# Context stages of a hybrid RWKV and convolution backbone: ScalarE reads each projection bank twice, VectorE works from a second SBUF tile

## The chip, the cores and the metric

The program runs on one core of one Trainium2 chip. The metric is the device time of one execution in microseconds (us), as the median of several runs. In the text TensorE is also called PE, VectorE DVE, ScalarE ACT, GpSimd POOL and SyncE SP, as the profile calls them. PEld is the loading of weights into TensorE, which overlaps its matmuls.

## The reference

The network has two layers over 512 latent tokens and 256 context tokens of width 1024. Layer 0 is the one that the change touches. It mixes tokens by a two-directional linear recurrence (RWKV-7), beside a short gated convolution. Layer 1 is a convolution module with a long kernel. What matters here of layer 0:

```python
def centred_shift(x):
    p = jnp.pad(x, ((0, 0), (1, 1), (0, 0)))
    return 0.5 * (p[:, :-2] + p[:, 2:])
...
    r = r + (centred_shift(r) - r) * mu_rkv[0]
    k = k + (centred_shift(k) - k) * mu_rkv[1]
    v = v + (centred_shift(v) - v) * mu_rkv[2]
...
    rc, kc, vc, zac, bc, cc, xc, zbc = jnp.split(hc @ w_in, EVEN_SPLITS, axis=-1)
    yac, S_f, S_b = rwkv_seq(rwkv_prep(hc, rc, kc, vc, *rw), zero, zero, r_k, lnx_w, lnx_b, ctx_out)
    r, k, v, za, bg, cg, xb, zb = jnp.split(h @ w_in, EVEN_SPLITS, axis=-1)
    ya, _, _ = rwkv_seq(rwkv_prep(h, r, k, v, *rw), S_f, S_b, r_k, lnx_w, lnx_b, True)
    y = jnp.concatenate([ya.astype(h.dtype) * jax.nn.silu(za), yb * jax.nn.silu(zb)], axis=-1) @ w_out
```

So each of the projections r, k and v is mixed with its left and right neighbour in time: (1 - mu) times itself plus mu/2 times each neighbour. The gate za goes through x * sigmoid(x).

## The kernel before, in words

All of layer 0 works on pairs of heads: 16 heads of 64 channels make 8 pairs of 128 channels, one channel to a partition, with time along the free dimension. A projection of one pair over the 512 latent tokens is 24 matmuls into one PSUM bank (8 blocks of the width, each as high times high, high times low and low times high of a number split in two fp32r parts). Over the 256 context tokens it is 24 shorter ones.

The work runs in 12 stages, `for s in range(12)` near the end of the function. Stages 0 to 3 are the context stages: each runs the recurrence of two head pairs over the context. Stages 4 to 11 do one head pair each over the latents. A stage holds a serial chain over chunks of 64 tokens (`chain_ctx`, `chain_lat`), and a string of letters, `STAGE`, says in what order the work for later stages is written beside it. K and V project k and v of the next two pairs (`prep_ctx`, `project`). L and H prepare the inputs of the recurrence (`light`, `heavy`). S and M invert the small triangular systems (`solve` on VectorE, 31 dependent steps; `merge` on TensorE, tile names mgc and mgl, which needs the result of `solve` in the tiles kdmc and amc, or kdml and aml). F fills in work that only later stages need: `fills` projects r and the gate za of the 8 pairs, by the tables `FILL_R` and `FILL_Z`, and sends them to DRAM.

The order that each engine runs in is not the written one. A scheduler lists the instructions of each engine by its own estimates of when they are ready, and every engine then runs its list strictly in that order. In a list a name ends in what it stands for: plv7 is the PSUM bank of v of pair 7 over the latents, pcv7 the same over the context, plr7 is r, pza7 the gate, pac30 and pal11 score blocks of a state, c2 the third context state and l0 the first latent state.

The change touches two helpers.

- `shifted` (lines 440 to 446) empties the bank of a projection. ScalarE writes (1 - mu) times the bank into the result tile (line 442). Then VectorE twice adds mu/2 times the bank, shifted by one column to the right and to the left (lines 443 and 445). These two read the bank again, so the bank is free after the second of them. `project` calls it once for the context bank, if there is one, and once for the latent bank.
- `gate` (lines 902 to 909) makes z * (1 + tanh(z / 2)): ScalarE reads the bank for the tanh (line 907), VectorE reads the bank again and multiplies (line 908).

The banks of projections alternate between two, mm0 and mm1 (`ps_mm`), so a projection can start when the one before the last has been emptied. The tile with the tag O has one buffer. In the latent stages it holds the output of a state. Before that the modulation's weights pass through it, fetched by `rest`, which counts its calls in `mv["n"]`: there are 17 calls, all of them before the context stages begin. The gate's tile gz also has one buffer, and is free again when its copy to DRAM has landed. These copies are queued on POOL.

Of the kernel before, what the change touches and what calls it, by code (L numbers as in the profile page):

```python
# [10 lines left out]
AF = mybir.ActivationFunctionType  # L11
ALU = mybir.AluOpType
# [6 lines left out]
SEQ = 512  # L19
# [33 lines left out]
def kernel(ctx: ExitStack, tc: tile.TileContext, I: dict, out: bass.AP):  # L53
    nc = tc.nc
    V, S, G, T = nc.vector, nc.scalar, nc.gpsimd, nc.tensor
# [111 lines left out]
    def ps_mm(name):  # L167
        flip["mm"] ^= 1
        return ps.tile([P, 512], F32, tag=f"mm{flip['mm']}", name=name)
# [17 lines left out]
    def w(tag, name, dt=F32):  # L187
        return wk.tile([P, SIZE.get(tag, 512)], dt, tag=tag, name=name, bufs=NBUF.get(tag, 1))
# [4 lines left out]
    def small(name, shape):  # L193
        return cvp.tile(shape, F32, tag=name, name=name)

    omu, hmu, hka, oka = (small(n, [P, k]) for n, k in (("omu", 24), ("hmu", 24), ("hka", 8), ("oka", 8)))
# [232 lines left out]
    def load_w(cb, name):  # L429
        lo_for(name)  # L430
        src = w_in[:, cb * P : (cb + 1) * P].rearrange("(k p) c -> p k c", p=P)
        return [w_half(src[:, 4 * b : 4 * b + 4, :], f"{name}{b}") for b in range(2)]

    def proj(wt, o, h):
        for kt in range(KT):
            ks = slice(kt % 4 * P, kt % 4 * P + P)
            wh, wl = wt[kt // 4]
            mm3(o, wh[:, ks], wl[:, ks], h[0][:, kt, :], h[1][:, kt, :], kt == 0, kt == KT - 1)

    def shifted(pl, res, p, which):  # L440
        j, n = which * 8 + p, pl.shape[1]
        S.activation(res, pl, AF.Copy, scale=omu[:, j : j + 1])
        V.scalar_tensor_tensor(out=res[:, 1:n], in0=pl[:, 0 : n - 1], scalar=hmu[:, j : j + 1],
                               in1=res[:, 1:n], op0=ALU.mult, op1=ALU.add)
        V.scalar_tensor_tensor(out=res[:, 0 : n - 1], in0=pl[:, 1:n], scalar=hmu[:, j : j + 1],
                               in1=res[:, 0 : n - 1], op0=ALU.mult, op1=ALU.add)

    def project(p, which, rc=None, between=None):
        nm = "rkv"[which] + str(p)
        wt = first_w.pop(nm) if nm in first_w else load_w(which * 8 + p, nm)  # L450
        if rc is not None:
            pc = (ps_at if nm in ("k0", "k1", "v0", "v1") else ps_mm)("pc" + nm)[:, :CTX]
            proj(wt, pc, (hch, hcl))
            shifted(pc, rc, p, which)
            if between:
                between()
        pl = ps_mm("pl" + nm)
        proj(wt, pl, hlat)
        flip["at"] ^= 1
        tag = ("cg", "yb")[flip["at"]]  # L460
        rl = cvp.tile([P, SEQ], F32, tag=tag, name="l" + nm)
        shifted(pl, rl, p, which)
        nc.gpsimd.dma_start(psp[p, which], rl)
# [438 lines left out]
    def gate(p, cb, nm):  # L902
        wt = load_w(cb + p, f"{nm}{p}")
        pz = ps_mm(f"p{nm}{p}")
        proj(wt, pz, hlat)
        g = cvp.tile([P, SEQ], F32, tag="gz", name=f"g{nm}{p}")
        S.activation(g, pz, AF.Tanh, scale=0.5)
        V.scalar_tensor_tensor(out=g, in0=g, scalar=1.0, in1=pz, op0=ALU.add, op1=ALU.mult)
        return g

    def finish(st):
# [21 lines left out]
    def fill(p):  # L933
        project(p, 0)
        gz = gate(p, 24, "za")
        nc.gpsimd.dma_start(psp[p, 3], gz)
# [39 lines left out]
    mv = {"n": 0}  # L976
# [49 lines left out]
    def fills(x):  # L1026
        for p in range(8):
            if FILL_R[p] == x:
                project(p, 0)
            if FILL_Z[p] == x:  # L1030
                gz = gate(p, 24, "za")
                nc.gpsimd.dma_start(psp[p, 3], gz)
# [24 lines left out]
    for s in range(12):  # L1057
# [11 lines left out]
        for x in STAGE[(s >= 2) + (s >= 4)]:  # L1069
# [25 lines left out]
            elif x == "C":  # L1095
                conv_branch(s - 3, st["anchor"])
                if s == 10:
                    rs.close()
                    op = rs.enter_context(tc.tile_pool(name="op", bufs=1, reuse_waits="tile", side="right"))
                    env["lo"] = V  # L1100
        if s == 3:
# [3 lines left out]
                                   op0=ALU.add, op1=ALU.mult)  # L1105
# [35 lines left out]
    with ExitStack() as l1:  # L1141
# [14 lines left out]
        def dense(name):  # L1156
            flip["mm"] = (flip["mm"] + 1) % 4
            return bank(name, ("mm0", "mm1", "uh0", "uh1")[flip["mm"]])
# [159 lines left out]
        for m in range(4):  # L1318
            mv = lp.tile([P, 4], F32, tag="mv", name=f"mv{m}", bufs=2)
# [3 lines left out]
            for q in range(2):  # L1323
                V.tensor_scalar(out=cres[m][q], in0=cres[m][q], scalar1=mv[:, 0:1], scalar2=mv[:, 3:4],
                                op0=ALU.subtract, op1=ALU.mult)
# [12 lines left out]
        for j in range(16):  # L1338
            c0 = 2 * EC + j * P
            src = w1_in[:, c0 : c0 + P].rearrange("(k p) c -> p k c", p=P)  # L1340
            pz = dense(f"pz{j}")
# [21 lines left out]
        for n in range(2):  # L1363
# [10 lines left out]
            for j in range(16):  # L1374
                if j % 2 == 0:
                    src = w2[j * P : (j + 2) * P, sl].rearrange("(a p) c -> p a c", p=P)
# [4 lines left out]
            for m in range(4):  # L1381
# [6 lines left out]
                if n == 0:  # L1388
                    V.tensor_tensor(out=sv, in0=acc[m], in1=gn, op=ALU.mult)
                    V.tensor_scalar(out=ssq[:, 2:3], in0=ssq[:, 0:1], scalar1=1.0 / D, scalar2=RMS_EPS,  # L1390
                                    op0=ALU.mult, op1=ALU.add)
# [87 lines left out]
```

## Time and profile before

| what | value |
|---|---|
| median of 3 runs | 1378.45 us (1374.93 to 1384.68) |
| the profiled execution's own time | 1377.51 us |
| its span, from the first to the last instruction | 1375.7 us |
| mean TensorE clock granted | 0.994 of full speed |
| TensorE, VectorE, ScalarE, GpSimd busy | 1315.9, 985.7, 743.1, 127.3 us |
| context stages with the first latent preparation, about | 150 to 470 us of the span |

The span is 1.8 us shorter than the execution's own time. What is worked out from the trace is set against the profiled execution, which lies 0.94 us under the median. A page of the profile gives each engine's busy time, and a chain that is followed back from the last instruction. The views of the trace used below are the waits (who waited for whom, how long, how often), the timeline of one engine (start, duration, what, and in square brackets the idle time before it and what ended it), the durations of one source line (smallest, median and largest, in ns), and windows (busy time of each engine in a stretch).

### The profile page before, as it was taken

The page shows a single profiled execution, that of the slowest core. Times are in us where ns is not written, and L with a number is a line of the kernel's source. Part 1 is how long each engine was busy: PE and PEld are TensorE (multiplying, and loading weights), DVE is VectorE, ACT ScalarE, POOL GpSimd, SP SyncE. Part 2 cuts the span into 40 slices and gives each one's busy share as a digit, 9 for nine tenths or more (in the row PEclk, how much of TensorE's full clock was granted, in tenths as well). Part 3 has the DMA queues.
Part 4 walks back from the last instruction along what each step waited for, and adds up shares of the span by engine and source line. Part 5 has one row for each costly group of instructions (what it writes and reads, how often), then busy time and mean ns, then how long its engine had stood idle before and what let it go on. Part 6 is the DMA issues. An engine that isn't in the chain of part 4 may idle for free.

```text
span 1375.7 us, 29697 instructions
## 1 busy us (share of the span) xinstructions
PE 1315.9 (96%) x11925; PEld 974.2 (71%) x11925; DVE 985.7 (72%) x2304; ACT 743.1 (54%) x1509; POOL 127.3 (9%) x263
## 2 busy tenths in 40 slices
PE   6999999999999999999999989999999999999998
PEld 2657677777667766666666666687787787788886
DVE  5857889767999699999999988458653653644323
ACT  6456466445765576675756745548741431654222
POOL 4142200001101010101101000010000000000000
PEclk9999999999999999999999999999999999999999
DMA  9965522222323322223222221678521321233232
GB/s 332 274 218 199 161 63 72 92 76 72 98 92 107 100 63 65 86 65 90 68 73 85 70 73 48 199 260 294 189 82 42 122 81 42 64 119 94 92 102 82
DMA packets 139754, 158.54 MB, mean 115 GB/s; under 512 B 15503, under 2 KB 104223, under 8 KB 139497
## 3 DMA queue, kind: packets, MB, share of 16 engines
q1 hardware_dynamic: 123152, 106.47, 24.9%
q0 software_dynamic: 15856, 49.12, 10.9%
q8 instruction: 93, 1.52, 0.5%
q10 hardware_dynamic: 608, 1.06, 0.2%
q14 instruction: 45, 0.37, 0.1%
HBM read 138.33 MB, written 18.28 MB: 114 GB/s over the span
## 4 chain that ended last, share of the span: by engine, by line
PE 49%; DVE 11%; ACT 7%; issue 4%; DMA 3%; POOL 0%; SPq 0%; DVEq 0%; ACTq 0%; POOLq 0%
PE pu L58 13%; PE pz L58 6%; PE f L58 6%; PE pxb L58 3%; PE o L58 3%; PE uh L58 3%; PE pcg L58 3%; DVE E L693 2%; PE pzb L58 1%; PE zol L58 1%; PE onl L58 1%; PE pc L58 1%; PE px L58 1%; DMA wr<-in_ev_w_out_dram 1%; PE plr L58 1%
## 5 line engine op out<-in xcount | busy, mean ns | idle before, releaser
L58 PE MATMUL o<-wh,y 128*128 128x512 f32 x248 | 79.7, 396 | 0.0
L752 DVE TENSOR_TENSOR xtmpl<-Xl,Yl 128x126 f32<-128x126 f32 (+22 forms) x248 | 62.6, 252 | 3.1
L754 DVE TENSOR_TENSOR Yl<-Yl,xtmpl 128x126 f32<-128x126 f32 (+22 forms) x248 | 62.5, 252 | 2.8
L1292 ACT CAST ah<-a 64x512 fp32r<-64x512 f32 x32 | 19.8, 618 | 74.1 <-DVE a L1287 73.7
L58 PEld LDWEIGHTS uh<-UV,BKt 128*64 128x64 f32 x704 | 26.4, 137 | 38.6 <-ACT UV L881 27.9
L58 PEld LDWEIGHTS o<-wh,y 128*128 128x128 f32 x248 | 46.2, 188 | 9.4
L58 PE MATMUL o<-wl,y 128*128 128x512 f32 x124 | 49.6, 400 | 1.5 <-DVE wl L131 1.5
L58 PE MATMUL pal<-ARl,BKl 64*128 64x128 f32 x512 | 43.9, 290 | 5.9 <-DVE E L693 2.6
L881 ACT COPY UV<-uh 64x128 f32<-64x128 f32 x128 | 33.2, 260 | 27.6 <-PE uh L58 25.3
L131 DVE TENSOR_TENSOR wl<-wr,wh 128x1024 fp32r<-128x1024 f32 x28 | 34.2, 1223 | 19.1 <-ACT wh L130 18.9
L1287 DVE TENSOR_TENSOR a<-pu,a 128x512 f32<-128x512 f32 x16 | 11.0, 690 | 49.5 <-PE pu L58 47.2
L58 PE MATMUL uh<-UV,BKt 128*64 128x64 f32 x704 | 36.6, 232 | 10.2 <-ACT UV L881 4.9
L58 PEld LDWEIGHTS pal<-ARl,BKl 64*128 64x128 f32 x512 | 34.5, 187 | 15.8 <-issue 6.3
L693 DVE TENSOR_TENSOR E<-pal,maskE 128x512 f32<-128x512 f32 x64 | 42.9, 686 | 0.4 <-PE pal L58 0.2
L1244 DVE SCALAR_TENSOR_TENSOR pr<-px,dbe,What 119x512 f32<-119x512 f32 x32 | 22.6, 746 | 26.6 <-PE px L58 26.6
L130 ACT CAST wh<-wr 128x1024 fp32r<-128x1024 f32 x28 | 29.6, 1056 | 18.9 <-DMA wr<-in_ev_w_out_dram 9.7
L58 PEld LDWEIGHTS uh<-Ol,E 64*64 64x64 f32 x512 | 20.3, 133 | 25.8 <-ACT Ol L874 23.9
L888 DVE SCALAR_TENSOR_TENSOR Hl<-uh,PCl,HPl 128x64 f32<-128x64 f32 x112 | 26.2, 276 | 13.2 <-ACT UV L881 5.0
L754 DVE TENSOR_TENSOR Yc<-Yc,xtmpc 128x126 f32<-128x126 f32 (+22 forms) x124 | 31.5, 254 | 3.2
L752 DVE TENSOR_TENSOR xtmpc<-Xc,Yc 128x126 f32<-128x126 f32 (+22 forms) x124 | 31.5, 254 | 3.1
L842 ACT ACTIVATE HPl<-Hl,PCl 128x64 f32<-128x64 f32 x96 | 28.1, 340 | 9.4 <-DVE Hl L888 8.4
L58 PEld LDWEIGHTS zol<-Hl,ARl 64*64 64x64 f32 x448 | 18.0, 134 | 20.8 <-DVE Yl L754 5.9
(1003 smaller groups left out, 4278.7 us busy)
## 6 DMA issues: line engine op xcount, KB each, us to landing
wr<-in_ev_w_out_dram SPq DMA_DIRECT2D x28, 512.0 KB, 5.2
mwr<-in_mod_w_dram POOLq DMA_DIRECT2D x28, 256.0 KB, 4.1
wrv<-in_ev_w_in_dram SPq DMA_DIRECT2D x16, 256.0 KB, 3.5
ectx<-in_mod_w_dram POOLq DMA_DIRECT2D x16, 256.0 KB, 4.2
wrr<-in_ev_w_in_dram SPq DMA_DIRECT2D x16, 256.0 KB, 2.8
wrza<-in_ev_w_in_dram SPq DMA_DIRECT2D x16, 256.0 KB, 2.9
wrcg<-in_ev_w_in_dram SPq DMA_DIRECT2D x16, 256.0 KB, 2.9
wrxb<-in_ev_w_in_dram SPq DMA_DIRECT2D x16, 256.0 KB, 3.1
```

Of the source, the lines that this page charges most:

```text
L58: env["pe"] = T.matmul(o, lhsT, rhs, start=start, stop=stop)
L130: S.copy(hi, raw)
L131: env["lo"].tensor_tensor(out=lo, in0=raw, in1=hi, op=ALU.subtract)
L693: st["ev"].append(V.tensor_tensor(out=E[:, h, z * NLAT + c0 : z * NLAT + c0 + m, :], in0=pas[h], in1=maskE[:, z * (1 + h) : z * (1 + h) + ...
L752: V.tensor_tensor(out=tv, in0=X[:, :i, i : i + 1].to_broadcast([P, i, m]), in1=Y[:, i : i + 1, c0:].to_broadcast([P, i, m]), op=ALU.mult)
L754: V.tensor_tensor(out=Y[:, :i, c0:], in0=Y[:, :i, c0:], in1=tv, op=ALU.add)
L842: S.activation(t[:, z, :], H[:, z, :], AF.Copy, scale=st["PC"][z][:, i : i + 1])
L881: u_ = S.copy(UV[ZR[1 - h], i : 2 * nch - i : 2 * nch - 1 - 2 * i, ZR[h]], uh[ZR[1 - h], 0:2, :])
L888: h_ = V.scalar_tensor_tensor(out=Hn[:, z, :], in0=uh[:, 2 + z, :], scalar=PC[z][:, i : i + 1], in1=HP[:, z, :], op0=ALU.mult, op1=ALU.add)
L1244: V.scalar_tensor_tensor(out=pr[s][:NPROD], in0=px[s][:NPROD], scalar=dbe[:, 0:1], in1=What[:, n * 512 : n * 512 + 512], op0=ALU.add, op1= ...
L1287: V.tensor_tensor(out=a, in0=pp[1], in1=a, op=ALU.mult)
L1292: S.copy(ahl[s][hr], a[hr])
```

## The change

From the seventeenth call of `rest` on, that is in the context stages, `shifted` has ScalarE read the bank a second time. It writes mu/2 times the bank into a second tile in the one buffer of tag O, and VectorE adds that tile, shifted by one column each way, with two plain additions. VectorE no longer reads the bank. Likewise `gate` has ScalarE copy the bank of za to the second tile, and VectorE multiplies from there. The projections and gates before this point, and the gates zb of the latent stages, stay as they were.

```diff
     def shifted(pl, res, p, which):
         j, n = which * 8 + p, pl.shape[1]
         S.activation(res, pl, AF.Copy, scale=omu[:, j : j + 1])
-        V.scalar_tensor_tensor(out=res[:, 1:n], in0=pl[:, 0 : n - 1], scalar=hmu[:, j : j + 1],
-                               in1=res[:, 1:n], op0=ALU.mult, op1=ALU.add)
-        V.scalar_tensor_tensor(out=res[:, 0 : n - 1], in0=pl[:, 1:n], scalar=hmu[:, j : j + 1],
-                               in1=res[:, 0 : n - 1], op0=ALU.mult, op1=ALU.add)
+        if mv["n"] < 17:
+            V.scalar_tensor_tensor(out=res[:, 1:n], in0=pl[:, 0 : n - 1], scalar=hmu[:, j : j + 1],
+                                   in1=res[:, 1:n], op0=ALU.mult, op1=ALU.add)
+            V.scalar_tensor_tensor(out=res[:, 0 : n - 1], in0=pl[:, 1:n], scalar=hmu[:, j : j + 1],
+                                   in1=res[:, 0 : n - 1], op0=ALU.mult, op1=ALU.add)
+            return
+        sh = w("O", f"sh{which}{p}{n}")[:, :n]
+        S.activation(sh, pl, AF.Copy, scale=hmu[:, j : j + 1])
+        V.tensor_tensor(out=res[:, 1:n], in0=sh[:, 0 : n - 1], in1=res[:, 1:n], op=ALU.add)
+        V.tensor_tensor(out=res[:, 0 : n - 1], in0=sh[:, 1:n], in1=res[:, 0 : n - 1], op=ALU.add)
...
         S.activation(g, pz, AF.Tanh, scale=0.5)
-        V.scalar_tensor_tensor(out=g, in0=g, scalar=1.0, in1=pz, op0=ALU.add, op1=ALU.mult)
+        src = pz
+        if nm == "za" and mv["n"] == 17:
+            src = w("O", f"sh{nm}{p}")[:, :SEQ]
+            S.copy(src, pz)
+        V.scalar_tensor_tensor(out=g, in0=g, scalar=1.0, in1=src, op0=ALU.add, op1=ALU.mult)
         return g
```

In the built program 24 calls of `shifted` (8 over the context, 16 over the latents) and 8 gates have the second read. The scheduler, which now sees the banks freed by ScalarE, also lists other work in another order, on all engines, from the first of them to the end of the first convolution in stage 3. After that the orders are the same again. Three places follow, as they stand in the lists.

TensorE around the merge of the third context state, before the change (pac300 are score blocks, plv7 the last projection of v, mgc2 the merge):

```order
L58 MATMUL pcv7_3538<-hctx_122,wlv71_3534 128x256
L58 MATMUL pac3001_3597<-ARc30_3274,BKc30_3275 128x64
...
L58 MATMUL pac3000_3596<-ARc30_3274,BKc30_3275 128x64
L58 MATMUL zoc2_0_3744<-UV000_1218,ectx_123 64x64 x4
L58 MATMUL mgc2_3386<-amc2_3378,ectx_123 32x32 x32
L58 MATMUL plv7_3566<-hlh0_117,whv70_3527 128x512
...
L58 MATMUL mgc2_3386<-kdmc2_3377,Pmc2_3379 32x32 x32
L58 MATMUL plv7_3566<-hlh0_117,wlv70_3528 128x512
```

The same place of the change:

```order
L58 MATMUL pcv7_3578<-hctx_122,wlv71_3574 128x256
L58 MATMUL plv7_3608<-hlh0_117,whv70_3567 128x512
...
L58 MATMUL plv7_3608<-hlh0_117,wlv70_3568 128x512
L58 MATMUL mgc2_3422<-amc2_3414,ectx_123 32x32 x32
L58 MATMUL plv7_3608<-hlh1_447,whv71_3573 128x512
...
L58 MATMUL mgc2_3422<-kdmc2_3413,Pmc2_3415 32x32 x32
L58 MATMUL plv7_3608<-hlh1_447,whv71_3573 128x512
...
L58 MATMUL pac3001_3641<-ARc30_3310,BKc30_3311 128x64
```

Twelve matmuls of plv7 moved ahead of the merge, nine stand between its halves, and the score blocks moved behind it. The merge of the second context state moved in the same way.

ScalarE at the second copies, of the change (sh26512 is the second tile of v of pair 6 over 512 tokens; before, the rows of the sh tiles were not there):

```order
L442 ACTIVATE lv6_3559<-plv6_3534,omu_99 128x512
L615 ACTIVATE Pc31_3328<-Pc31_3328 128x528
L450 ACTIVATE sh26512_3561<-plv6_3534,hmu_100 128x512
L617 COPY PCc31_3333<-Pc31_3328 128x8
L648 COPY BKc31_3341<-BKc31_3341 64x8x64
L442 ACTIVATE vc3_3491<-pcv7_3578,omu_99 128x256
L771 COPY ectx_123<-kdmc2_3413 32x16x32 x2
L130 CAST whr21_3752<-wrr21_3751 128x512
L780 COPY Pmc2_3415<-mgc2_3422 32x512
L450 ACTIVATE sh27256_3604<-pcv7_3578,hmu_100 128x256
```

The second read of a bank need not stand right behind the first: it stands where the second tile is thought to be free.

VectorE at the end of the inversion of the first latent state, before the change (Xl1 is the transposed input of the next inversion, E110 a score block after its mask):

```order
L693 TENSOR_TENSOR E110_4729<-pal1111_4944,maskE_107 128x512
L752 TENSOR_TENSOR xtmpl0_4788<-Xl0_4786,Yl0_4787 128x70
L445 SCALAR_TENSOR_TENSOR lr7_5183<-plr7_5158,hmu_100,lr7_5183 128x511
...
L754 TENSOR_TENSOR Yl0_4787<-Yl0_4787,xtmpl0_4788 128x16
L746 STREAM_TRANSPOSE Xl1_5640<-Nt_111 128x32x32
L760 STREAM_TRANSPOSE kdml0_4853<-Yl0_4787 128x32x16
L761 STREAM_TRANSPOSE aml0_4854<-kdml0_4853 128x512
```

The same place of the change:

```order
L760 TENSOR_TENSOR Yl0_4843<-Yl0_4843,xtmpl0_4844 128x16
L131 TENSOR_TENSOR wlxb01_5300<-wrxb01_5298,whxb01_5299 128x512
L766 STREAM_TRANSPOSE kdml0_4909<-Yl0_4843 128x32x16
L699 TENSOR_TENSOR E110_4785<-pal1101_4988,maskE_107 128x512
L767 STREAM_TRANSPOSE aml0_4910<-kdml0_4909 128x512
L771 COPY E100_4207<-kdml0_4909 32x16x32 x2
L131 TENSOR_TENSOR wlbg00_5336<-wrbg00_5334,whbg00_5335 128x512
L452 TENSOR_TENSOR lr7_5245<-sh07512_5247,lr7_5245 128x511
L780 COPY Pml0_4911<-mgl0_4918 32x512
L699 TENSOR_TENSOR E110_4785<-pal1110_4999,maskE_107 128x512
```

The second addition for lr7, two of the masked blocks and the transposition Xl1 moved behind the last step of the inversion's transposition aml0, for which the merge of that state waits.

## The prediction

> **What bounds the kernel now.** I read the page's busy times first, then the chain that ended last, then the busy time of each engine in the stretch that the change touches.
>
> ```profile
> PE 1315.9 (96%) x11925; PEld 974.2 (71%) x11925; DVE 985.7 (72%) x2304; ACT 743.1 (54%) x1509; POOL 127.3 (9%) x263
> PE 49%; DVE 11%; ACT 7%; issue 4%; DMA 3%; POOL 0%; SPq 0%; DVEq 0%; ACTq 0%; POOLq 0%
> 150.00:470.00 320.00, 302.45 (x3236) 232.23 (x3235) 266.77 (x684) 186.55 (x382) 33.37 (x61) 0.99 0.31 92
> ```
>
> The first row is busy time by engine, the second the shares of that chain, the third the stretch from 150 to 470 us (length, then PE, PEld, DVE, ACT and POOL busy, the granted clock and the DMA share). TensorE sets the time. Its number of matmuls is not changed, so the edit can gain only what TensorE loses in this stretch: 320.00 - 302.45 = 17.55 us of idle time, and time lost at a lower clock. VectorE is busy 83% there and ScalarE 58%. So ScalarE has room on average, but both run strictly in order, and a wait is decided at its place. The waits of TensorE in the stretch name those places (total in us, how often, the longest):
>
> ```profile
> PE uh L58 <- ACT UV L817: 4.9, 8, 1.3
> PE mgc L58 <- DVE amc L761: 4.3, 4, 1.7
> ...
> PE lac L58 <- ACT ac L599: 1.2, 2, 0.6
> PE mgl L58 <- DVE aml L761: 1.1, 1, 1.1
> PE plv L58 <- DVE lv L445: 0.6, 1, 0.6
> ```
>
> Only the last of these rows, one wait of 0.6 us, is a projection that waits for VectorE to empty its bank. So the direct aim of the edit, a bank that is free sooner, is worth almost nothing. What is large are waits of the serial chain (uh for UV) and of the merges (mgc, mgl) for the inversion on VectorE. These the edit can reach only through the new order, and through the load that it puts on ScalarE and takes from VectorE.
>
> **The instructions themselves.** The next rows are durations of one line (smallest, median, largest in ns): ScalarE's read of a bank (L442, and the plain copy L948), VectorE's additions from a bank (L443), its multiplication of a gate from a bank (L908) and the same operation from SBUF (L625), and plain additions in SBUF (L131).
>
> ```profile
> L442 ACT ACTIVATE kc<-pck,omu x8: 453/468/475, 56.2 to 297.3; 128x256 f32<-128x256 f32 x8
> L442 ACT ACTIVATE lr<-plr,omu x8: 681/684/691, 168.5 to 444.4; 128x512 f32<-128x512 f32 x8
> L948 ACT COPY cg<-pcg x8: 568/580/588, 459.6 to 837.6; 128x512 f32<-128x512 f32 x8
> L443 DVE SCALAR_TENSOR_TENSOR kc<-pck,hmu,kc x8: 476/482/484, 56.9 to 297.8; 128x255 f32<-128x255 f32 x8
> L443 DVE SCALAR_TENSOR_TENSOR lr<-plr,hmu,lr x8: 741/746/750, 169.3 to 445.4; 128x511 f32<-128x511 f32 x8
> L908 DVE SCALAR_TENSOR_TENSOR gza<-gza,pza x8: 645/681/689, 185.4 to 404.1; 128x512 f32<-128x512 f32 x8
> L625 DVE SCALAR_TENSOR_TENSOR ac<-ac,kkc x8: 683/685/689, 116.4 to 318.4; 128x512 f32<-128x512 f32 x8
> L131 DVE TENSOR_TENSOR wlr<-wrr,whr x16: 642/685/694, 150.0 to 433.7; 128x512 fp32r<-128x512 f32 x16
> L131 DVE TENSOR_TENSOR y<-yr,y x30: 406/418/427, 869.1 to 971.3; 128x256 fp32r<-128x256 f32 x30
> ```
>
> Added on ScalarE: 16 second copies of 512 columns at 0.684, 8 of 256 at 0.468 and 8 gate copies at 0.580, that is 10.9 + 3.7 + 4.6 = 19.3 us. Saved on VectorE: 32 additions of 512 columns at 746 - 685 = 61 ns and 16 of 256 at 482 - 418 = 64 ns, that is 2.0 + 1.0 = 3.0 us; the 8 multiplications of the gates cost 681 ns from a bank and 685 from SBUF, so nothing there. An addition from the second tile is not in this trace as such. Its bounds are the two rows of each width (0.685 or 0.746); I take the lower, since the plain addition in SBUF is the nearer in kind. VectorE's 3.0 us lie spread over 320 us and under TensorE's work, so I book them only at the places below. If that cover were gone they would be worth 3.0 us at most.
>
> **The merge of the third context state.** First TensorE, then VectorE (start, duration, what, idle time before it).
>
> ```profile
> 319.76 2.00 PE L58 MATMUL pac<-ARc,BKc 64*128 64x64 f32 x32
> ...
> 323.18 1.20 PE L58 MATMUL mgc<-amc,ectx 32*32 32x32 f32 x64 [1.03 <-DVE amc L761]
> 324.94 0.77 PE L58 MATMUL plv<-hlh,whv 128*128 128x512 f32 x1 [0.56 <-DVE lv L445]
> 330.21 0.63 PE L58 MATMUL plv<-hll,whv 128*128 128x512 f32 x1
> 330.64 0.63 PE L58 MATMUL plv<-hlh,wlv 128*128 128x512 f32 x1
> 334.32 0.39 PE L58 MATMUL plv<-hll,whv 128*128 128x512 f32 x1
> 334.55 0.39 PE L58 MATMUL plv<-hlh,wlv 128*128 128x512 f32 x1
> ```
>
> ```profile
> 322.41 0.71 DVE L761 STREAM_TRANSPOSE amc<-kdmc 128x512 f32<-128x512 f32 x1
> ...
> 324.04 0.75 DVE L445 SCALAR_TENSOR_TENSOR lv<-plv,hmu,lv 128x511 f32<-128x511 f32 x1
> ```
>
> Two waits stand here, 1.03 + 0.56 = 1.59 us. In the new order 12 matmuls of plv7 come ahead of the merge, from 319.76 on where the score blocks began, at 334.55 - 334.32 = 0.23 us each: 2.76 us, to 322.5. The transposition amc ends at 322.41 + 0.71 = 323.1, so about 0.6 to 0.7 us of waiting is left, and the second wait is gone, as the bank is given back by ScalarE. **-0.9 us**. Bounds: -1.59 if VectorE reaches amc earlier, and 0 if plv7 waits for its bank in place of the merge: the second tile of v of pair 6 must itself first be free, which takes two additions of the tile before it on VectorE.
>
> **The clock.** The pairs of starts above are 330.64 - 330.21 = 0.43 us apart and then 0.23. In between TensorE came back to full speed, as the windows show (busy times as above, then the granted clock):
>
> ```profile
> 320.40:323.80 3.40, 2.37 (x73) 2.16 (x71) 3.36 (x6) 2.05 (x4) 0.71 (x2) 1.00 0.67 169
> 324.80:328.20 3.40, 3.26 (x37) 2.36 (x39) 2.76 (x5) 0.25 (x1) 0.56 (x1) 0.50 0.20 77
> 328.20:331.60 3.40, 3.40 (x46) 2.85 (x43) 0.69 (x1) 0.57 (x1) 0.00 (x0) 0.50 0.00 0
> ```
>
> A thin stretch (2.37 of 3.40 us busy) is followed by 6.8 us at a clock of 0.50. Some eleven matmuls of plv7 at 0.43 instead of 0.23 make 2.2 us lost. The new order puts full-sized matmuls into the thin stretch. Bounds: -2.2 if the slow stretch goes, +3.4 (half of 6.8) if it stays and another is set off elsewhere, 0 if it stays alone. I take half of the gain, **-1.1 us**, since the thin stretch becomes denser but does not vanish. The Trainium skill, "TensorE: Matmul & The Clock Gate", Part 1 on the clock gate, says that the array drops to half clock after an idle window of about 3.4 us, in a window that runs free of the program; the trace agrees with the length (two windows of 3.40) but not with idle, since the window before was 70% busy. By that rule taken strictly, 12 more matmuls in the window would end the slow stretch, and the whole 2.2 us would be saved: 1.1 us below my sum.
>
> **The merges of the second and the fourth state.**
>
> ```profile
> 240.10 2.00 PE L58 MATMUL pac<-ARc,BKc 64*128 64x64 f32 x32
> 243.77 1.20 PE L58 MATMUL mgc<-amc,ectx 32*32 32x32 f32 x64 [1.67 <-DVE amc L761]
> 393.26 1.20 PE L58 MATMUL mgc<-amc,ectx 32*32 32x32 f32 x64 [0.84 <-DVE amc L761]
> ```
>
> For the second, 12 matmuls of plv5 (2.76 us) come ahead in place of the score blocks (2.00): **-0.8 us**, bounds 0 and -1.67. For the fourth the order now has 15 matmuls of the last gate ahead rather than 8, 7 x 0.23 = 1.6 us of work, which covers the 0.84: **-0.8 us**, bounds 0 and -0.84. Work moved ahead is missing behind, and there the next in line is the chain's uh, whose 4.9 us of waits I leave as they are.
>
> **The end of stage 3.** TensorE's waits, then VectorE's rows that move:
>
> ```profile
> 441.32 1.16 PE L58 MATMUL pal<-ARl,BKl 64*128 64x128 f32 x16 [1.68 <-ACT BKl L642]
> 451.15 0.71 PE L666 MATMUL pbl<-ident,BKl 64*128 64x64 f32 x16 [0.58 <-ACT BKt L706]
> 454.74 1.20 PE L58 MATMUL mgl<-aml,E 32*32 32x32 f32 x64 [1.14 <-DVE aml L761]
> ```
>
> ```profile
> 446.22 0.69 DVE L693 TENSOR_TENSOR E<-pal,maskE 128x512 f32<-128x512 f32 x1
> 450.98 2.03 DVE L746 STREAM_TRANSPOSE Xl<-Nt 128x1024 f32<-128x1024 f32 x1
> ```
>
> Xl1 (2.03), two masked blocks (0.69 each) and one addition (0.685) now come behind aml0: it can end about 4 us sooner. But TensorE too has less ahead of the merge there: two groups of score blocks like the one at 451.15 (0.71 each) and part of pal (1.16), about 2.6 us. So the 1.14 us of waiting goes, and the rest of the sooner end is not used: **-1.1 us**, bounds -3.4 (all three waits) and 0 (if Xl1 is late next, for the second inversion).
>
> **What ScalarE pays.** The second copies stand in its queue ahead of the chain's copies. One such place:
>
> ```profile
> 211.92 0.68 ACT L442 ACTIVATE lk<-plk,omu 128x512 f32<-128x512 f32 x1
> 213.03 0.75 ACT L817 COPY UV<-zoc 64x256 f32<-64x256 f32 x2 [0.43 <-PE zoc L58]
> ```
>
> ScalarE had 0.43 us to spare; a second copy of 0.68 here makes UV about 0.25 us late, and uh behind it. By the new order four places have a second copy right ahead of a copy of the chain. Their bounds are 4 x 0.25 = 1.0 and, with a wait for the tile as long again as the missing time, 2.4 us; I take **+0.8**, as a copy of the chain is not always the last that TensorE waits for. The decay's matmuls (lac) now have one group of the projection ahead, not seven or eight; they wait 1.2 us now, and I add **+0.5**, bounds 0 and 1.2 (as much again).
>
> **Sum**, against the profiled execution's 1377.51: -0.9 - 1.1 - 0.8 - 0.8 - 1.1 + 0.8 + 0.5 = -3.4, so **1374.1 us**. That execution lies 0.94 under the median of the runs, which is less than their spread.
>
> **The rivals.**
>
> *The order only moves the waits.* What is put ahead of one merge is missing behind it; VectorE, 83% busy, delivers amc and aml when it did. For it: each new filler was a filler before. Against it: the slow clock after a merge is a real loss, not a wait in a sum. Then 1377.5 us.
>
> *ScalarE becomes the bound: slower.* The one buffer O lets a second copy start only when VectorE has done both additions of the tile before, and VectorE puts them behind steps of the inversion. ScalarE then stands at the head of its queue, with UV, cx and the gates' tanh behind it, for which uh and zoc of the serial chain wait. That decides where the additions come later than the next second copy is wanted, which is when projections follow each other at 24 x 0.23 = 5.5 us or faster while VectorE is in the inversion. If each second copy passes to TensorE in full, the price is the 19.3 us of ScalarE: 1396.8 us. Against it: ScalarE is idle 320 - 187 = 133 us in the stretch.
>
> *A slow clock elsewhere.* If waits of the new order thin out another window, 3.4 us are added and the 1.1 us is not gained: 1374.1 + 1.1 + 3.4 = 1378.6, up to 1384 with ScalarE's upper bound of 2.4 and the merges unchanged.
>
> *All of it goes.* If VectorE's lighter load and the fillers remove every wait of the stretch, 17.55 + 2.2 = 19.8 us: 1357.8 us. Against it: 4.9 us are the chain's own latency (uh for UV), which gets no shorter.
>
> *The gates don't come free.* One row speaks for a part of the edit doing nothing:
>
> ```profile
> 383.07 0.60 ACT L907 ACTIVATE gza<-pza 128x512 f32<-128x512 f32 x1 [3.82 <-DVE Yc L754]
> ```
>
> This tanh began long after ScalarE was free. If what holds it is the one buffer gz, the bank waits as before, and the copy only follows the tanh: +0.58 at worst, within the sum.
>
> **How the numbers follow.** Forecast 0.44, only moved 0.26, slow clock elsewhere 0.12, ScalarE the bound 0.12, all gone 0.06. The range takes at its low end the waits at the merges and the end of stage 3 (1.59 + 1.67 + 0.84 + 3.40 = 7.5), the chain's 4.9 and the clock's 2.2: 1377.5 - 14.6 = 1363 us. At its high end: nothing gained, ScalarE 2.4, lac 1.2 and the clock 3.4: 1377.5 + 7.0, rounded up to 1385 us. The two cases outside it hold 0.18. One per cent, 13.8 us, is about what a measurement of this kernel can tell from no change: faster by more needs nearly all idle time gone (0.06), slower needs ScalarE as the bound (0.12), 0.82 lies between.
>
> **What would show it.** Right: ScalarE's busy time up by 19 us and VectorE's down by 3, the wait of plv for lv gone, mgc's waits for amc at 2 us or less in place of 4.3, no half clock near 325 us. Wrong: uh waiting for UV well over 4.9 us, rows of the sh tiles on ScalarE with idle time ended by VectorE's additions, or a half clock at a new place.

## The result and the profile after

| | before | changed |
|---|---|---|
| median | 1379.19 us (10 runs, 1374.93 to 1384.68) | 1372.11 us (10 runs, 1367.69 to 1374.20) |
| profiled execution | 1377.51 us | 1372.10 us |
| mean granted clock over the runs | 0.992 (77 runs beside the kernels below) | 0.997 (10 runs) |

The ratio is 0.9943, with a 95% interval of 0.9929 to 0.9958: about 7 us faster. The forecast was a gain of 3.4 us, to 1374.1. The direction and the range held, the size was half of what came. In the profiled pair, against which the sum was set, the gain is 5.4 us. Two executions of several thousand us, one of the kernel before and one of the six stops below, are left out of all figures.

The page of the changed kernel, busy times and shares of the last chain, and the stretch from 150 to 470 us:

```profile
PE 1316.0 (96%) x11925; PEld 971.8 (71%) x11925; DVE 984.1 (72%) x2304; ACT 757.2 (55%) x1541; POOL 127.2 (9%) x263
PE 64%; DVE 15%; ACT 9%; DMA 6%; issue 5%; SPq 0%; POOL 0%; DVEq 0%; ACTq 0%; POOLq 0%
```

```profile
150.00:470.00 320.00, 308.30 (x3263) 235.23 (x3256) 267.50 (x688) 201.90 (x417) 33.37 (x61) 1.00 0.31 94
```

ScalarE is 14.1 us busier over the program and VectorE 1.6 us less, both somewhat under the sums of their instructions (19.3 and 3.0). TensorE does the same matmuls and is busy 5.85 us more in the same 320 us: so much of its idle time has gone from the window. Its waits in the stretch, in the view quoted before (total in us, how often, the longest):

```profile
PE mgc L58 <- DVE amc L767: 2.2, 4, 0.8
PE uh L58 <- ACT UV L823: 1.9, 6, 0.6
PE pal L58 <- DVE E L699: 1.2, 2, 0.8
PE zoc L58 <- DVE Hc L832: 1.2, 3, 0.5
PE pal L58 <- ACT BKl L648: 1.1, 1, 1.1
PE zoc L58 <- ACT cx L816: 1.1, 3, 0.6
```

The waits of mgc for amc have halved (4.3 to 2.2) and those of uh for UV have gone from 4.9 to 1.9. The waits of lac, of plv for lv and of mgl for aml are no longer listed. New is zoc waiting 1.1 us for ScalarE's copy cx, which is the chain's other copy. The timeline of TensorE at the merges of the second, third and fourth state and at the end of stage 3:

```profile
244.22 1.20 PE L58 MATMUL mgc<-amc,ectx 32*32 32x32 f32 x64 [0.39 <-DVE amc L767]
...
322.80 1.20 PE L58 MATMUL mgc<-amc,ectx 32*32 32x32 f32 x64 [0.39 <-DVE amc L767]
...
389.93 1.20 PE L58 MATMUL mgc<-amc,ectx 32*32 32x32 f32 x64 [0.68 <-DVE amc L767]
...
440.83 1.16 PE L58 MATMUL pal<-ARl,BKl 64*128 64x128 f32 x16 [1.14 <-ACT BKl L648]
445.85 0.49 PE L58 MATMUL pal<-ARl,BKl 64*128 64x128 f32 x4 [0.42 <-DVE E L699]
446.36 1.20 PE L58 MATMUL mgl<-aml,E 32*32 32x32 f32 x64
449.29 1.20 PE L58 MATMUL mgl<-kdml,Pml 32*32 32x32 f32 x64 [0.20 <-DVE Pml L780]
450.93 0.71 PE L672 MATMUL pbl<-ident,BKl 64*128 64x64 f32 x16 [0.43 <-DVE E L699]
454.26 0.71 PE L672 MATMUL pbl<-ident,BKl 64*128 64x64 f32 x16 [0.36 <-ACT BKt L712]
```

The brackets at the two middle merges have shrunk from 1.67 and 1.03 to 0.39. The windows around the third merge of the changed kernel (length, PE, PEld, DVE, ACT, POOL busy, clock):

```profile
321.70:325.10 3.40, 3.01 (x73) 2.34 (x72) 3.29 (x7) 2.50 (x5) 0.56 (x1) 1.00 0.28 81
325.10:328.50 3.40, 3.40 (x79) 2.47 (x77) 1.88 (x4) 1.34 (x3) 0.56 (x1) 1.00 0.49 155
```

TensorE is busy 3.01 of 3.40 us where it was 2.37, and the clock stays at 1.00. This execution has one half clock before its end, at a new place in the latent stages:

```profile
570.93:574.34 3.41, 2.17 (x80) 1.97 (x80) 3.18 (x7) 2.37 (x4) 0.57 (x1) 1.00 0.50 142
574.34:577.75 3.41, 3.41 (x25) 2.35 (x18) 3.32 (x9) 3.05 (x5) 0.00 (x0) 0.50 0.25 77
```

For the whole stretch, two landmarks that both kernels have in the same order, the first lwc and the transposition pgv, before and then changed:

```profile
108.90 0.48 PE L58 MATMUL lwc<-lorc,lwc0lwl 64*128 64x256 f32 x1
...
474.61 0.27 PE L1110 MATMUL pgv<-ident,ss 128*16 128x128 f32 x1
```

```profile
109.85 0.48 PE L58 MATMUL lwc<-lorc,lwc0lwl 64*128 64x256 f32 x1
...
470.24 0.27 PE L1120 MATMUL pgv<-ident,ss 128*16 128x128 f32 x1
```

Between them lie 365.71 and 360.39 us: 5.3 us are gained here, in this pair of executions. Before them 0.95 us is lost, where the programs don't differ.

### The profile page after: what moved, and what is told of

It is laid out like the page before. It is cut to its first block, busy times and chain, and to the rows that moved or that the text cites. A ratio compares the mean times of both kernels' runs of the same rounds, so it can differ in the third digit from the quotient of the medians.

```text
span 1370.3 us, 29726 instructions
## 1 busy us (share of the span) xinstructions
PE 1316.0 (96%) x11925; PEld 971.8 (71%) x11925; DVE 984.1 (72%) x2304; ACT 757.2 (55%) x1541; POOL 127.2 (9%) x263
## 4 chain that ended last, share of the span: by engine, by line
PE 64%; DVE 15%; ACT 9%; DMA 6%; issue 5%; SPq 0%; POOL 0%; DVEq 0%; ACTq 0%; POOLq 0%
PE pu L58 10%; PE pz L58 6%; PE f L58 6%; PE o L58 5%; PE uh L58 3%; PE pxb L58 3%; PE plv L58 3%; PE pcg L58 2%; PE pzb L58 2%; PE plk L58 2%; PE pza L58 2%; DVE E L699 2%; PE pcv L58 1%; PE plr L58 1%; PE pac L58 1%
## 5 line engine op out<-in xcount | busy, mean ns | idle before, releaser
L894 DVE SCALAR_TENSOR_TENSOR Hl<-uh,PCl,HPl 128x64 f32<-128x64 f32 x112 | 26.3, 276 | 12.2 <-ACT UV L887 5.0
```

The source lines that it names most:

```text
L894: h_ = V.scalar_tensor_tensor(out=Hn[:, z, :], in0=uh[:, 2 + z, :], scalar=PC[z][:, i : i + 1], in1=HP[:, z, :], op0=ALU.mult, op1=ALU.add)
```

## The experiments

Each kernel ran beside the kernel before; the ratio is to the runs beside it, the means are against all 77 runs of before. A result lists for each run the clock granted on average, so a time can be split. Over the 203 runs of all kernels, in deviations from the mean of each kernel, a run was 0.71 us longer for each us by which its clock fell short of full over 1375 us (correlation 0.79). The clock's part of a difference from the kernel before is worked out with that: 0.71 x 1375 us x the difference in mean clock. It is an estimate by regression, so tenths of it mean little.

| kernel | median, us | ratio to before, 95% | mean clock | mean against before | of it clock | rest |
|---|---|---|---|---|---|---|
| before (77 runs) | 1378.99 | | 0.9921 | | | |
| the change | 1372.11 | 0.9943 [0.9929, 0.9958] | 0.9973 | -7.4 | -5.0 | -2.3 |
| mixings only | 1373.68 | 0.9962 [0.9947, 0.9976] | 0.9962 | -5.1 | -3.9 | -1.2 |
| gates only | 1376.89 | 0.9989 [0.9971, 1.0007] | 0.9938 | -1.5 | -1.7 | +0.1 |
| second copies unread | 1390.59 | 1.0088 [1.0067, 1.0109] | 0.9847 | +12.3 | +7.3 | +5.0 |
| merges first | 1376.80 | 0.9979 [0.9967, 0.9992] | 0.9925 | -2.7 | -0.3 | -2.3 |
| before, filled | 1377.84 | 0.9994 [0.9978, 1.0010] | 0.9961 | -1.3 | -3.8 | +2.5 |
| unread, three fewer | 1380.24 | 1.0017 [1.0000, 1.0035] | 0.9909 | +1.7 | +1.2 | +0.5 |
| addition on GpSimd | 1383.39 | 1.0039 [1.0022, 1.0056] | 0.9927 | +4.9 | -0.5 | +5.4 |
| merges first, filled | 1374.32 | 0.9974 [0.9957, 0.9990] | 0.9971 | -3.9 | -4.8 | +0.9 |
| latents only | 1372.47 | 0.9960 [0.9943, 0.9978] | 0.9968 | -5.4 | -4.6 | -0.8 |
| another second tile | 1387.33 | 1.0063 [1.0042, 1.0084] | 0.9900 | +9.1 | +2.1 | +7.0 |
| the change, six stops | 1382.11 | 1.0019 [1.0007, 1.0031] | 0.9975 | +3.2 | -5.2 | +8.4 |
| the change, twelve stops | 1387.17 | 1.0053 [1.0034, 1.0073] | 0.9967 | +7.8 | -4.4 | +12.2 |

**Mixings only.** The gates keep the form of before.

```diff
-        if nm == "za" and mv["n"] == 17:
+        if False:
```

> Only the 24 mixings have the second read by ScalarE, the gates are as before. Its order has the merges of the second and third context state behind 12 matmuls of plv5 and plv7, as the whole change has. Theory A (the gain is the new order at these two merges, which the bank freed by ScalarE allows, and the slow clock that went with the old one): 4 to 7 us under before, no half clock near 325 us, and mgc's waits for amc near 2 us. Theory B (VectorE's lighter load): 3 of the about 7 us at most from this part alone, spread over the stretch. Theory C (any new order would do, chance): no relation, -3 to +3.

About 5 us faster, within what theory A said and more than theory B's 3. Its profile has no half clock near 325 us, and these waits:

```profile
PE mgc L58 <- DVE amc L767: 2.2, 4, 0.8
PE uh L58 <- ACT UV L823: 1.8, 6, 0.6
```

They are those of the whole change. The mixings carry most of it. The profile does have a half clock at a new place of the stretch, 377.16 to 380.57 us, behind a wait of 2.28 us at pal.

**Gates only.**

```diff
-        if mv["n"] < 17:
+        if True:
```

> Only the 8 gates have the copy by ScalarE, the mixings are as before; the order at the merges of the second and third context state is that of before. Theory A: within 1.5 us of before, mgc's waits for amc at 4 us, and a half clock after the third merge as before. Theory B: within 0.5 us, as the multiplication takes VectorE as long from SBUF. Theory C: -3 to +3.

Not told apart from before by its interval. The order at the merges is the old one, and so are the waits; here the second merge waited 1.77 us, and the half clock stands at that merge, not at the third as in the profile of before:

```profile
244.19 1.92 PE L58 MATMUL mgc<-amc,ectx 32*32 32x32 f32 x64 [1.77 <-DVE amc L767]
```

```profile
239.91:243.32 3.41, 2.51 (x37) 2.22 (x35) 3.41 (x6) 1.93 (x5) 0.12 (x1) 1.00 0.57 154
243.32:250.15 6.83, 5.96 (x109) 4.84 (x111) 5.17 (x10) 1.80 (x4) 0.97 (x2) 0.50 0.26 79
```

The windows here and in the next experiment are cut where the half clock begins and ends. In all the traces it lasts 3.41 us or a multiple of that, but for the one at the end of a run.

**Second copies unread.** ScalarE does all that the change has it do, VectorE works from the bank.

```diff
         S.activation(sh, pl, AF.Copy, scale=hmu[:, j : j + 1])
-        V.tensor_tensor(out=res[:, 1:n], in0=sh[:, 0 : n - 1], in1=res[:, 1:n], op=ALU.add)
-        V.tensor_tensor(out=res[:, 0 : n - 1], in0=sh[:, 1:n], in1=res[:, 0 : n - 1], op=ALU.add)
+        V.scalar_tensor_tensor(out=res[:, 1:n], in0=pl[:, 0 : n - 1], scalar=hmu[:, j : j + 1],
+                               in1=res[:, 1:n], op0=ALU.mult, op1=ALU.add)
+        V.scalar_tensor_tensor(out=res[:, 0 : n - 1], in0=pl[:, 1:n], scalar=hmu[:, j : j + 1],
+                               in1=res[:, 0 : n - 1], op0=ALU.mult, op1=ALU.add)
...
             S.copy(src, pz)
+            src = pz
```

> ScalarE makes all second copies, but nobody reads them: VectorE adds and multiplies from the bank as before, and still frees it. This is the price of ScalarE's 19.3 us without what they buy. The merges stand in the order of before. Theory A: 0 to 2 us over before. Theory B: 0 to 2 us over before too. A third, that ScalarE's time passes to the chain in part and the gain of the whole change is net of it: 3 to 8 us over before, with uh waiting for UV well over 4.9 us.

Both main theories missed: it is 12 us slower, over the 8 us of the third too. Nor is it the way that the third had it: uh waits 4.3 us for UV in this kernel's stretch, less than before. ScalarE's queue near 192 us and TensorE's answer show what happened (start, duration, what, idle before):

```profile
191.82 0.69 ACT L442 ACTIVATE lr<-plr,omu 128x512 f32<-128x512 f32 x1
192.40 0.68 ACT L450 ACTIVATE sh<-plr,hmu 128x512 f32<-128x512 f32 x1
192.97 0.37 ACT L818 COPY cx<-zoc 128x256 f32<-128x256 f32 x1
```

```profile
193.40 0.27 PE L58 MATMUL zoc<-cx,ectx 64*64 64x64 f32 x1 [2.50 <-ACT cx L818]
```

```profile
191.67:195.08 3.41, 1.68 (x38) 1.48 (x38) 3.38 (x7) 1.65 (x4) 0.53 (x1) 1.00 0.28 77
195.08:212.14 17.06, 17.06 (x182) 14.54 (x179) 10.92 (x33) 8.04 (x18) 0.56 (x2) 0.50 0.08 32
212.14:215.55 3.41, 3.41 (x30) 2.67 (x30) 0.80 (x5) 2.31 (x6) 0.00 (x0) 1.00 0.02 5
```

A second copy, with other work of ScalarE, stands ahead of the chain's copy cx. TensorE waits 2.5 us, is busy only 1.68 of 3.41 us, and then runs at half clock for 17 us, though it is busy throughout. This trace has half clock at four other places of the stretch as well. From here on theory A became theory A': the new order pays mostly through the granted clock.

**Merges first.** The whole change, with plv5 and plv7 held behind the first half of the merge.

```diff
+        mv["mg" + nm] = env["pe"].ins
...
-        proj(wt, pl, hlat)
+        with tc.issue_after(mv["mgc" + nm[1:2].translate({53: 49, 55: 50})]) if nm in ("v5", "v7") else nullcontext():
+            proj(wt, pl, hlat)
```

> The whole change, but the latent projections of v of pairs 5 and 7 are held behind the first half of the merge of the second and third context state, so that TensorE has there the order of before, with VectorE's load and the banks freed as in the change. Theory A: 3 to 5 us of the change's 7 are lost (about 1375 to 1377), mgc waits for amc 3.5 to 4.5 us in all, and a half clock may come back near 325 us. Theory B: the gain stays, 1371 to 1373.

4.7 us of the change's 7.4 (by the means) are lost, as theory A said. But the split says more: the clock falls back to that of before, and the rest is that of the change (-2.3 in both). So by this split what the order at the merges is worth is the clock. Its one profile has mgc waiting 3.6 us for amc, as expected, but no half clock in any context stage: the three that it has before its end lie at 33, at 576 to 586 and at 644 us. So this trace doesn't show how the clock was lost, and in which place the other runs had theirs isn't known.

**Before, filled.** One useless fp32 matmul ahead of each context merge, into the merge's own bank.

```diff
+        for _ in range(1 if nm[0] == "c" else 0):
+            mm(pg, R1.rearrange("p a b -> p (a b)")[:, 0:128], R1.rearrange("p a b -> p (a b)"), True, True)
         for q in range(16):
```

> The kernel before, with one more matmul of 128x512 in fp32 ahead of each merge of a context state. It reads kdmc, so it can start only when the first transposition is done, and runs while TensorE waits for amc; it writes to the merge's own bank, where the merge then overwrites it. It does no useful work and frees nothing. Theory A' (the gain is for the larger part the granted clock, which falls after a thinned-out window): the clock rises and 1.5 to 4 us are gained, though work is added. Theory W (the gain is the waits that are gone): no gain, 0 to 4 us slower, as four matmuls of about 0.9 us are added.

The clock rises as A' said, from 0.992 to 0.996, but the time doesn't move clear of its interval: the gain of 1.5 to 4 us was missed. The trace has both sides. The filler takes 1.13 us in each of four merges, and its waits for kdmc take the place of those for amc:

```profile
324.75 1.13 PE L58 MATMUL mgc<-kdmc 128*128 128x512 f32 x2 [0.42 <-DVE kdmc L760]
326.65 1.20 PE L58 MATMUL mgc<-amc,ectx 32*32 32x32 f32 x64
```

```profile
PE mgc L58 <- DVE kdmc L760: 2.3, 4, 0.8
```

4 x 1.13 + 2.3 - 4.3 = 2.5 us are added, the size of the rest of +2.5 in the table, against 3.8 of clock.

**Merges first, filled.** The two edits together.

> The change with the merges held ahead of plv5 and plv7, and in addition the filling matmul ahead of each context merge. Against the same kernel without it (1376.8 at a clock of 0.993): Theory A': the clock returns to 0.996 or more and 2 to 4 us are gained, 1373 to 1375. Theory W: 0 to 3 us slower, 1377 to 1380.

Against merges first alone the clock goes from 0.9925 to 0.9971 and the median from 1376.80 to 1374.32, as A' said; the intervals of the two overlap, so it is the clock that is clear here, not the time. By the means the clock's part is 4.5 us and the rest is 3.2 slower (the fillers again). The fillers stand at the context merges only. This points to them as the place where merges first lost its clock, although its one profile doesn't show it.

**Unread, three fewer.** Without the second copies of r of pairs 0 and 1 and of the gate of pair 0.

```diff
-        S.activation(sh, pl, AF.Copy, scale=hmu[:, j : j + 1])
+        if which or p > 1:
+            S.activation(sh, pl, AF.Copy, scale=hmu[:, j : j + 1])
...
-            S.copy(src, pz)
+            if p:
+                S.copy(src, pz)
             src = pz
```

> As the kernel with the second copies that nobody reads, but without the three second copies of the first fill (r of pairs 0 and 1, the gate of pair 0), which stood ahead of the chain's copy cx near 192 us, where TensorE then waited 2.5 us and the clock was at half for some 18 us. 21 second copies are left. Theory A': most of the 11 us come from that one place and the half clock behind it: 1380 to 1384, clock above 0.990. The rival, that every copy costs its share of ScalarE's time: 3 of 24 copies less gives back 1.5 us, about 1389.

10.4 us come back for three copies of 2 us in all (2 x 0.68 + 0.58), within what theory A' said, and the half clock behind 195 us is gone. What a second copy costs is decided by its place, not by its length.

**Addition on GpSimd.**

```diff
-        V.tensor_tensor(out=res[:, 1:n], in0=sh[:, 0 : n - 1], in1=res[:, 1:n], op=ALU.add)
+        G.tensor_tensor(out=res[:, 1:n], in0=sh[:, 0 : n - 1], in1=res[:, 1:n], op=ALU.add)
```

> The whole change, with the first of the two additions from the second tile on GpSimd in place of VectorE (24 of 48 additions, 14 us less on VectorE). If VectorE's queue sets the waits that are left at the merges: 1 to 3 us under the change, 1369 to 1371. If GpSimd's additions are much longer than VectorE's, the second tile is held longer, ScalarE's second copies wait for it, and the chain's copies behind them: 2 to 15 us over the change.

11 us over the change, the size of the second case. GpSimd's addition takes 1.2 us where VectorE's took 0.69, and mgc waits for amc as long as before the change, though VectorE has 24 additions less:

```profile
L451 POOL TENSOR_TENSOR lr<-sh,lr x8: 1083/1180/1706, 176.8 to 454.0; 128x511 f32<-128x511 f32 x8
```

```profile
PE mgc L58 <- DVE amc L767: 4.4, 4, 1.4
PE zoc L58 <- DVE Hc L832: 3.6, 3, 2.0
```

But VectorE itself now waits for GpSimd, 7.3 us in all, and at the third state right ahead of the transposition of the inversion:

```profile
326.36 0.69 DVE L452 TENSOR_TENSOR lv<-sh,lv 128x511 f32<-128x511 f32 x1 [0.98 <-POOL lv L451]
```

So this kernel doesn't tell what a lighter VectorE alone would give.

**Latents only.** The 8 context banks as before, almost no other row moved.

```diff
-        if mv["n"] < 17:
+        if mv["n"] < 17 or n == CTX:
```

> The change without the second read of the 8 context banks of 256 columns (VectorE adds from these as before): ScalarE has 3.7 us less, VectorE 1.0 us more, the order is nearly that of the change. If ScalarE's load costs the change something in waits of the chain: 0.5 to 2 us under the change, 1370 to 1371.6. If only order and clock count: within 1 us of the change, clock 0.996 to 0.998.

0.4 us from the change by the medians (1.9 by the means) and not told apart from it: these 3.7 us of ScalarE's load cost nothing that shows in the change's order.

**Another second tile.**

```diff
-        sh = w("O", f"sh{which}{p}{n}")[:, :n]
+        sh = w("tmp", f"sh{which}{p}{n}")[:, :n]
...
-            src = w("O", f"sh{nm}{p}")[:, :SEQ]
+            src = w("tmp", f"sh{nm}{p}")[:, :SEQ]
```

> The change with the second tile taken from the three rotating buffers tmp in place of the one buffer O, which takes away the second copy's wait for VectorE's additions (0.6 us in the change's trace) but gives a new order on every engine. If the one buffer holds ScalarE up: 1 to 3 us under the change. Theory A': the waits gain nothing, and the time goes with the granted clock of the new order: 1369.5 plus 0.7 us for each us by which the clock falls short over the span (0.001 of the clock is 1.4 us).

15 us over the change. In the new order the second copy of a bank of r stands on ScalarE behind the preparation of a state's inputs, and TensorE waits for that bank:

```profile
440.10 0.79 PE L58 MATMUL plr<-hlh,whr 128*128 128x512 f32 x1 [3.92 <-ACT sh L450]
```

The one buffer O held ScalarE up by 0.6 us only (the change's trace). This is the rival of the slower side in another form: a second copy that comes late holds the bank that it was to free, and cx (4.5 us of waits here) comes late behind it. Whether the buffers themselves held it wasn't separated from the order.

**Stops in a dense part.** Both kernels add memsets on GpSimd between two groups of matmuls and use none of them: 12 at six places, or 5 at twelve.

```diff
+                for i in range(12):
+                    g_ = G.memset(stats[:, 0, 0, 0:2], 0.0)
+                    if not i:
+                        tc.add_manual_dep(g_.ins, held_by.ins.name, need, reason="behind the group before")
...
+                    tc.add_manual_dep(e_.ins, g_.ins.name, need, reason="held")
```

> The change, with TensorE stopped six times in the part near 1200 to 1280 us where it is otherwise 100% busy with matmuls of 128x512: each stop waits for a row of 12 small memsets on GpSimd, about 2.5 us by estimate, 15 us in all. The stops add work that the result doesn't use. Theory A' (a long stop halves the clock after it): 20 to 35 us over the change, clock below 0.99. If stops cost only themselves: what their own lengths in the trace sum to, about 15.

> The same with twelve stops of 5 memsets, about 1.25 us each by estimate, one to every 5.4 us of matmuls, so about the same sum as six long ones. Theory A': the windows stay filled, the clock stays at 0.996 or more, and the stops cost only what they are long, about 15 us. If any stop sets off the half clock: 30 us and more.

The first missed its aim: part of the next group slipped into the stop, and it came out as two short ones, 0.95 and 0.26 us, 10 us over the change in all. So long stops remain untried. Both kernels show short ones, and both keep the clock. In the second they came out at 0.8 to 0.9 us for the 1.25 of the estimate. The first of them, its window, and the whole part:

```profile
1213.10 0.50 PE L58 MATMUL pz<-h1h,wz4h 128*128 128x512 f32 x1 [0.84 <-POOL stats L1357]
```

```profile
1210.00:1213.40 3.40, 2.56 (x11) 1.82 (x11) 0.91 (x2) 1.53 (x3) 0.50 (x5) 1.00 0.54 154
1195.00:1300.00 105.00, 94.20 (x422) 73.47 (x421) 39.42 (x47) 42.58 (x60) 7.00 (x62) 1.00 0.29 86
```

10.8 us of idle time cost 15 us, so each stop costs some 0.4 us more than its bracket, but not the clock: a window busy 2.56 of 3.40 us amid full ones didn't lower it.

## Why the prediction was right, and where it was not

**What bounds.** Right: only TensorE's losses in the stretch could be won, and 5.3 us of them were, in the profiled pair.

**The merges.** The second and third were right in kind and a little small: -1.3 and -1.2 us (brackets 1.67 to 0.39, and 1.03 + 0.56 to 0.39) for -0.8 and -0.9. The fourth was wrong, -0.2 for -0.8: the bracket went from 0.84 to 0.68 only. The end of stage 3 gave 1.14 + 0.42 + 0.20 + 0.43 + 0.36 = 2.55 for 3.40, -0.85 for -1.1, with mgl's wait for aml gone as said, and three new waits of 0.20 to 0.43 in its place.

**ScalarE.** The step "the second copies stand in its queue ahead of the chain's copies", +0.8, had the wrong sign in the change: uh waits 3.0 us less for UV and zoc 1.1 us more for cx. The uh waits I had left "as they are". Why uh waits less was not tried by itself; with merges first it still waits 3.0 us, of 4.9 before. Latents only shows that in this order 3.7 of the 19.3 us cost nothing measurable; the kernel with unread copies shows that in another order the copies cost 12 us. I priced the copies by their length, and took the spare time of one row for all places. The upper bound of 2.4 us is also a slip: four places at twice the missing 0.25 us make 2.0.

**lac.** "I add +0.5": the waits, 1.2 us, are gone, but about as much was lost beside them. Before, each matmul of lac ran side by side with one of lwc; in the new order most of them run one after the other (before, then changed):

```profile
306.23 0.48 PE L58 MATMUL lac<-lorc,lwc3lwl 64*128 64x256 f32 x1
306.24 0.48 PE L58 MATMUL lwc<-lorc,lwc3lwl 64*128 64x256 f32 x1
```

```profile
305.16 0.70 PE L58 MATMUL lac<-lorc,lwc3lwl 64*128 64x256 f32 x2
...
305.84 0.48 PE L58 MATMUL lwc<-lorc,lwc3lwl 64*128 64x256 f32 x1
```

The eight matmuls took 1.07 us (306.23 to 307.30, where the next begins) and take 1.73 (305.16 to 306.89), and so too near 227 us: 1.3 us in all.

**The sum of the waits** was -2.3 us and the rest beside the clock came out as -2.3 in the means of the runs. That is luck. In the profiled pair the waits fell by 5.9 us (17.3 to 11.4, the sums of that view over 150 to 470 us), 3.0 of them at uh, for which nothing was booked. Between the two landmarks, before and then changed:

```profile
108.90:474.61 365.71, 348.11 (x3562) 264.89 (x3562) 299.71 (x759) 211.71 (x432) 43.43 (x80) 0.99 0.33 101
```

```profile
109.85:470.24 360.39, 348.62 (x3563) 263.94 (x3562) 298.10 (x759) 225.63 (x464) 43.44 (x80) 1.00 0.33 103
```

TensorE is idle 17.6 us before and 11.8 after, and busy for as long. So in this pair the 5.3 us are idle time, and what the slow stretch cost is made up for by matmuls that occupy TensorE longer in the new order, of which lac and lwc are one case. The prediction has no term for that.

**The clock** is the term that was mis-sized: "I take half of the gain, -1.1 us". By the regression it was worth 5 us in the mean of the runs (0.9921 to 0.9973). I read one profiled execution as if the slow stretch near 325 us were the place and its 2.2 us the price. That execution had a clock of 0.994, better than the mean of before, and two more slow stretches, at 642 and 823 us. Other executions of kernels with the old order have theirs at other merges (gates only at 243 us; unread, three fewer, at 244 and at 329 us). How thin a window is doesn't decide it alone. The changed kernel's half clock at 574 us followed a window busy 2.17 us. In the execution before, the first of these windows was followed by the half clock and the second was not:

```profile
321.37:324.78 3.41, 1.97 (x80) 1.65 (x78) 3.33 (x7) 1.91 (x4) 0.56 (x1) 1.00 0.56 139
573.95:577.36 3.41, 2.17 (x21) 1.50 (x19) 3.39 (x7) 1.30 (x3) 0.57 (x1) 1.00 0.44 129
```

The Trainium skill, "TensorE: Matmul & The Clock Gate", Part 1, says that the window runs free of the program, so that a run differs from the next; the spread of 0.988 to 0.996 over the runs of before agrees. Its rule of an idle window does not: the 3.41 us right ahead of the slow stretches were busy 1.68 (second copies unread), 1.97 (before) and 2.51 us (gates only).

**The signs named beforehand.** The wait of plv for lv is gone, and so is the half clock near 325 us. mgc's waits came to 2.2 us, where 2 or less was named, ScalarE rose by 14.1 us for 19 and VectorE fell by 1.6 for 3. Of the signs against, a half clock at a new place appeared, at 574 us.

Shown by experiment: the mixings carry most of the gain (5.1 of 7.4 us by the means); the order at the two merges is worth 4.7 us, and the mean clock goes down with it and comes back with the fillers; 3.7 us of ScalarE's load in this order cost nothing that shows. By the regression alone: that the 4.7 us are all clock. The traces add an indication only, since each kernel has one profile. Of the five with the change's order at the merges and all additions on VectorE out of the buffer O (the change, mixings only, latents only, the two with stops), one has a half clock between 150 and 470 us; of the five with the order of before and no fillers (before, gates only, second copies unread, three fewer, merges first), four have. Not separated: what VectorE's lighter load gives. Merges first keeps it and is 2.7 us under before, but has the rest of the new order too. Nor was it tried how long a single stop must be to halve the clock.

## What to carry to other kernels

Where TensorE sets the time, look at the mean clock of several runs before pricing a wait: here 0.005 of the mean clock went with some 5 us, where one trace had suggested 1 to 2. A bank that is freed by the less loaded engine is worth what it lets a scheduler put ahead of a wait; and a copy added to an in-order queue costs by the instruction that stands behind it, not by its own length. A single profile of a kernel with half-clock stretches shows one draw of where they fall, not their price.

## What the runs showed of the hardware

- The half clock lasted 3.41 us or a multiple of it: 6.83 (before, 324.78 to 331.61), 10.24 (merges first, from 576.19) and 17.06 us (second copies unread, 195.08 to 212.14, with TensorE busy throughout). In these and gates only, the 3.41 us ahead of it were busy 1.63 to 2.51 us, not idle; a window busy 2.17 us in the execution before was not followed by it. Within the kernels a us of clock shortfall went with 0.71 us of time.
- Matmuls whose weights are 64 x 128 ran side by side where two of different tiles alternated in the order: lac and lwc started 0.01 us apart (306.23 and 306.24), and eight took 1.07 us, against 1.73 mostly one after the other.
- Rows of ScalarE overlap: two reads of a bank of 0.69 us start 0.58 us apart (191.82 and 192.40), one reason why 19.3 us of added rows raised its busy time by 14.1.
- On GpSimd the addition of 128x511 took 1.18 us (median) and VectorE's, in the same place of the change, 0.69.
